# A hybrid decoder step: two small log1p series moved from GpSimd to VectorE, a pair's logarithms issued together, and the planner's lag within an engine set to zero

## The chip, the core and the metric

The kernel runs on one core of a Trainium2 chip. The core has a matrix engine (TensorE; PE in the profile, with its weight loads as PEld), a vector engine (VectorE; DVE), a scalar engine for activation functions (ScalarE; ACT), a general engine (GpSimd; POOL), and a sync engine (SyncE; SP) which here only issues DMAs. Each engine works through its own instructions in program order; they are tied together by semaphores. The metric is the device time of one execution in microseconds (us).

## The reference

One inference step of a two-layer recurrent decoder, for a prompt of 512 tokens and 8 sample tokens, 520 columns in all, width 1024. Layer 0 has two branches, an RG-LRU and a Mamba-2 SSD; layer 1 is an HGRN2. Three places of the reference matter here.

```python
# RG-LRU: constants per channel from a_lam
log_a = -LRU_C * r * jax.nn.softplus(-lam.astype(F32))
a = jnp.exp(log_a)
u = jnp.sqrt(-jnp.expm1(2.0 * log_a)) * (gi * x)
...
# SSD: step sizes per token and head
dt = jax.nn.softplus(b_dt.astype(F32) + b_dt_bias.astype(F32))
acs = jnp.cumsum(dtc * a_neg.reshape(G_B, hg), axis=2)
...
# HGRN2: forget gate and its sums over time
g = jnp.logaddexp(jnp.log(lb), jnp.log1p(-lb) + jax.nn.log_sigmoid(fx))
bcum = jnp.cumsum(gs.reshape(Bsz, H_C, qc, DK_C), axis=2).reshape(Bsz, H_C, ns, ss, DK_C)
```

softplus(x) is max(x, 0) + log1p(exp(-|x|)). The kernel computes the log1p of z = exp(-|x|) by the series 2 (s + s^3/3 + s^5/5 + ... + s^17/17) with s = z / (z + 2).

## The kernel before

All matrix products are made in split single precision: a weight tile and the activations are each cut into a high and a low part (`whi`/`wlo`, `whir`/`wlor`, `xnh`/`xnl`), and three matmuls of 128x128 by 260 columns replace one. A projection tile (128 output rows, 520 columns, 48 matmuls) accumulates in one of two PSUM buffers of the tag `mm`; the next but one tile must wait until an evacuation has emptied it. Everything small goes through four more PSUM banks (`ax`).

Nothing is issued in the order in which it is written. Each call records an operation in a plan (`Plan.record`), with its engine (some copies and scalings may go to ACT or DVE), a cost from a table and a due time: the position of the main matmuls at that place of the program, shifted by `side(...)`. `urgency` pulls the due time of everything that a main matmul depends on to 38.78 us before that matmul. `order` is then a list scheduler: at each step the engine that is free first takes the operation with the earliest due time among those whose predecessors have ended by the cost table. What an operation's end is reckoned to cost its successors is the lag in `release`: `SYNC` (0.12 us) for all but PE to PE, and for PE instructions fed by other engines the spare that `later(...)` sets. `together(...)` puts a gate ahead of a group: no operation of the group is planned before all writes to the named views are done. In hardware the queues run in the planned order, and true dependences wait on semaphores.

The order of the work around the change:

- `norm0` normalizes the input into `xnh`/`xnl`. Behind a gate on the first four tiles of `xnl` come the small tables: `buffers`, `tables` and, later, `dt_tables` and `lower_bounds`.
- `tables` makes the LRU constants. From `a_lam` (8 columns, in `lamt`) ACT takes the absolute value and one exponential at 1/32 of the argument; POOL squares five times (`accurate_exp`), runs the series (`log1p_of`, whose reciprocal alone is on DVE) and makes `c4` and `nc4`.
- The tiles `ax0` to `ax7` are projected. `evac_ax` evacuates each with ACT, convolves it over time on DVE (`conv`), with a POOL and three DVE steps more for the 8 sample columns, and `gates` follows: split `xg`, twelve matmuls `g`, two tanh, then `lt` and `lr`, whose ACT instructions take `nc4` and `c4` as scale and bias. `lru` runs the recurrence on DVE.
- `ssd_start` projects dt (`dt_project`, planned behind `ax7`), takes |dt| and its exponential on ACT, runs the series on 80 columns, and makes `dt` and `dA`. The matmuls `acs` sum `dA` over time. `acsT` goes through DRAM and comes back as `acy`, from which the SSD chunks start. All of `ssd_start` and `lru_out` stands under `later(4.0)`.
- In layer 1 the heads come in eight pairs. For each pair f and v are projected (by a seven-product scheme from the second pair on, tiles `sm` and `sg`), then `decay` for both heads, then q, in the pairs 2, 4 and 6 a chunk of the output projection (`o`), then g. `samples` and `head` of a pair run beside the next pair's projections.
- `decay` takes for each head a logarithm on ACT into `b`, a scan on DVE, eight exponentials on ACT into `qe` and `kd`. Logarithm and exponential lie in different activation tables, so a change between them needs an ACT_TABLE_LOAD. q's evacuation multiplies into `qe` and so waits for the exponentials. `b` of a head lies where the head of the same parity of the previous pair keeps its output `og`; the last readers of that are the cast and the subtraction into `ohl`, at the end of `head`.

In the profile lines, `at__1738` is `at_`, `l1a` is the buffer of `t`, `b`, `kd` and `qe`, and nearly all instructions carry line 520, where the plan issues them, so they are told apart by tile.

Of the kernel before, what the change touches and what calls it, by code (L numbers as in the profile page):

```python
# [29 lines left out]
NH = 16  # L30
# [165 lines left out]
def _meet(a, b):  # L196
    return a[2] < b[3] and b[2] < a[3] and a[0] < b[1] and b[0] < a[1]
# [12 lines left out]
class Plan:  # L210
# [44 lines left out]
        self.spare = keep  # L255

    @contextmanager
    def together(self, *views):

        self.gate = self.barrier([o for v in views for box, o, w in v.buf.acc if w and _meet(box, v.box())])  # L260
        yield
        self.gate = None

# [91 lines left out]
    def order(self):  # L355
# [17 lines left out]
        def release(op, t):  # L373
            todo = [(op, t)]
            while todo:
                p, t_ = todo.pop()
                for s, hard in p.succ:
                    if hard:
                        lag = SYNC if p.forms and not ("pe" in p.forms and "pe" in s.forms) else 0
                        if "pe" in s.forms and p.taken != "pe":  # L380
                            lag += s.spare
                        s.ready = max(s.ready, t_ + lag)
                    s.wait -= 1
                    if not s.wait:
                        offer(s, todo)
# [155 lines left out]
def hybrid_decode_step_kernel(ctx: ExitStack, tc: tile.TileContext, I, O, mode="both"):  # L541
# [44 lines left out]
    def tt(out, a, b, op, eng=dve):  # L586
        eng.tensor_tensor(out=out, in0=a, in1=b, op=op)
# [365 lines left out]
    flag = ctile([1, 1], "flag", I32)  # L953
    fl = ctile([128, 4], "fl")

    def log1p_of(z, n, lo):

        t = htmp[:, lo:lo + 4 * n].rearrange("p (a b) -> p a b", a=4)
        s, s2, q, r = t[:, 0], t[:, 1], t[:, 2], t[:, 3]
        ts(s, z, 2.0, ADD, eng=pool)  # L960
        dve.reciprocal(q, s)
        tt(s, z, q, MUL, pool)
        tt(s2, s, s, MUL, pool)
        ts(q, s2, 1.0 / 17.0, MUL, 1.0 / 15.0, ADD, pool)
        for c in (13, 11, 9, 7, 5, 3, 1):
            tt(q, q, s2, MUL, pool)
            ts(q, q, 1.0 / c, ADD, eng=pool)
        tt(r, q, s, MUL, pool)
        ts(r, r, 2.0, MUL, eng=pool)
        return r  # L970

    def accurate_exp(t, k):

        fn(t, t, AF.Exp, scale=1.0 / (1 << k))
        for _ in range(k):
            tt(t, t, t, MUL, pool)

    def buffers():

# [11 lines left out]
    def tables():  # L991
        pool.memset(triu, 1.0)
        select(triu, [[1, 128]], 0, -1, 0.0)

        act.activation(lamt[:, 0], P1(56, 8), AF.Abs)
        ts(lamt[:, 0], lamt[:, 0], -1.0, MUL, eng=pool)
        accurate_exp(lamt[:, 0], 5)
        l1p_ = log1p_of(lamt[:, 0], 8, 320)
        ts(lamt[:, 1], P1(56, 8), -1.0, MUL, 0.0, MAX, pool)
        tt(lamt[:, 1], lamt[:, 1], l1p_, ADD, pool)  # L1000
        ts(c4, lamt[:, 1], -4.0, MUL, eng=pool)
        ts(nc4, lamt[:, 1], 4.0, MUL, eng=pool)
        ts(hbias, P1(40, 16), 0.5, MUL, eng=pool)
        ts(hcn, P2(64, 16), 0.5, MUL, eng=pool)

        ts(P1(64, 60), P1(64, 60), 0.5, MUL, eng=pool)
# [53 lines left out]
    with plans[-1].together(xnl[:, 3]):  # L1060
        with side(12.0):
            buffers()
            tables()
        with side(25.0):
            dt_tables()
        with side(40.0):
            lower_bounds()
# [157 lines left out]
    def ssd_start():  # L1225
        dt_project()
        act.activation(dt_z, dt_raw, AF.Abs)
        fn(dt_z, dt_z, AF.Exp, scale=-1.0)
        lg_ = log1p_of(dt_z, 80, 0)
        ts(dt, dt_raw, 0.0, MAX, eng=pool)  # L1230
        tt(dt, dt, lg_, ADD, pool)
        tt(dA.rearrange("p (i h) -> p i h", i=5), dt.rearrange("p (i h) -> p i h", i=5),
           bc(aneg.unsqueeze(1), [128, 5, NH]), MUL, pool)
        ps = grab("acs")
        with block():
            pe.matmul(ps[:, 0:64], lhsT=triu, rhs=dA[:, :64], start=True, stop=True)
            pe.matmul(ps[:, 64:128], lhsT=ones, rhs=dA[:, :64], start=True, stop=True)
        copy(at_[:, 0:2, :], ps[:, :128].rearrange("p (a b) -> p a b", a=2))
        ts(nacs[:, :64], acs, -1.0, MUL)
        tt(edt, alast, acs, SUB)  # L1240
        ps = grab("acsT")
        with block():
            pe.transpose(ps[:64, :128], acs, ident)
            pe.transpose(ps[:16, 128:256], dt[:, 64:80], ident)
            pe.transpose(ps[:16, 256:384], dA[:, 64:80], ident)
        copy(acsT, ps[:64, :128])
        copy(sdt[:, 0, :], ps[:16, 248:256])
        fn(sdt[:, 1, :], ps[:16, 376:384], AF.Exp)
        fn(edt, edt, AF.Exp)
        fn(eal, alast, AF.Exp)  # L1250
        sp.dma_start(out=acsT_d, in_=acsT)
        sp.dma_start(out=sdt_d, in_=sdt.rearrange("h a b -> h (a b)"))
        for e in range(2):
            sp.dma_start(out=sfm[e * 64:(e + 1) * 64].rearrange("p j a b -> p j (a b)"),
                         in_=sdt_d.rearrange("(j e) c -> e j c", e=2)[e].partition_broadcast(64))
# [6 lines left out]
                lru(0)  # L1262
    with side(LRU_LATE):
        lru(4)
    with side(DT_LATE), plans[-1].later(4.0):
        ssd_start()
        lru_out()

# [342 lines left out]
    def layer1_fast():  # L1611
# [174 lines left out]

        def decay(hd):

            with plans[-1].together(H[hd]["t"], H[hd + 1]["t"]):
                for e in (hd, hd + 1):  # L1790
                    fn(H[e]["b"][:, :T], H[e]["t"][:, :T], AF.Ln, scale=ch[:, e:e + 1], bias=fb[:, e:e + 1])
            for e in (hd, hd + 1):
                d, p = H[e], e % 2
                b = d["b"][:, :T]
                dve.tensor_tensor_scan(out=b, data0=smask, data1=b, initial=0.0, op0=MUL, op1=ADD)
                b4 = c4v(b)
                last, mid = b4[:, :, CH - 1:CH], b4[:, :, CH // 2 - 1:CH // 2]
                kd, qe = A[:, 2080 + p * T:2080 + (p + 1) * T], A[:, 3104 + p * T:3104 + (p + 1) * T]
                w = small[:, p * 4:p * 4 + 4]
                d.update(kd=kd, qe=qe, w=w)  # L1800
                nm = small[:, 20 + p * 4:24 + p * 4]
                ts(nm.unsqueeze(2), mid, -1.0, MUL)
                for c in range(NCH):
                    cs = slice(c * CH, (c + 1) * CH)
                    fn(qe[:, cs], b[:, cs], AF.Exp, bias=nm[:, c:c + 1])
                    fn(kd[:, cs], b[:, cs], AF.Exp, scale=-1.0, bias=mid[:, c])
                stt(kd, d["t"][:, :T], 1.0, kd, SUB, MUL)
                tt(w.unsqueeze(2), last, mid, SUB)
                tt(w[:, :NCH - 1].unsqueeze(2), w[:, :NCH - 1].unsqueeze(2), mid[:, 1:], ADD)
                fn(w, w, AF.Exp)  # L1810
                ts(w[:, NCH - 1:], w[:, NCH - 1:], cneg[:, e:e + 1], MUL)
# [453 lines left out]
```

## Time and profile before

| | us |
|---|---|
| median of three runs | 1055.54 |
| lowest and highest | 1050.91, 1056.95 |
| profiled execution, device time | 1052.58 |
| its span, first to last instruction | 1050.9 |
| ACT_TABLE_LOAD beside the first, number and each | 36, 1.283 |
| granted TensorE clock, mean over the span | 0.994 |

The profile is of one execution. Timeline rows give start, duration, engine, line, operation, output and inputs with sizes, and in brackets how long the engine stood idle just before and what released it. [...]

### The profile page before, as it was taken

The page shows a single profiled execution, that of the slowest core. Times are in us where ns is not written, and L with a number is a line of the kernel's source. Part 1 is how long each engine was busy: PE and PEld are TensorE (multiplying, and loading weights), DVE is VectorE, ACT ScalarE, POOL GpSimd, SP SyncE. Part 2 cuts the span into 40 slices and gives each one's busy share as a digit, 9 for nine tenths or more (in the row PEclk, how much of TensorE's full clock was granted, in tenths as well). Part 3 has the DMA queues.
Part 4 walks back from the last instruction along what each step waited for, and adds up shares of the span by engine and source line. Part 5 has one row for each costly group of instructions (what it writes and reads, how often), then busy time and mean ns, then how long its engine had stood idle before and what let it go on. Part 6 is the DMA issues. An engine that isn't in the chain of part 4 may idle for free.

```text
span 1050.9 us, 21517 instructions
## 1 busy us (share of the span) xinstructions
PE 1023.1 (97%) x8427; PEld 1000.0 (95%) x8427; DVE 832.6 (79%) x1705; ACT 630.8 (60%) x1482; POOL 139.4 (13%) x241
## 2 busy tenths in 40 slices
PE   9989899999999999999999999999999999999995
PEld 8989899899999999999999999999999999999995
DVE  6789788998996656697989759698598979868853
ACT  6588876654673222365676726678268685764553
POOL 4635854100000000001000000001000000100000
PEclk9999999999999999999999999999999999999998
DMA  9712254336586223553353433433434443553311
GB/s 285 246 30 92 81 166 141 122 110 191 188 257 213 89 98 117 153 203 90 98 149 109 142 91 108 139 100 113 122 90 139 124 116 111 137 180 121 121 41 45
DMA packets 129957, 138.45 MB, mean 132 GB/s; under 512 B 13704, under 2 KB 111128, under 8 KB 129832
## 3 DMA queue, kind: packets, MB, share of 16 engines
q1 hardware_dynamic: 129464, 136.64, 42.6%
q8 instruction: 68, 1.11, 0.4%
q10 hardware_dynamic: 160, 0.30, 0.1%
q14 instruction: 41, 0.34, 0.1%
q0 software_dynamic: 224, 0.06, 0.0%
HBM read 111.71 MB, written 25.44 MB: 131 GB/s over the span
## 4 chain that ended last, share of the span: by engine, by line
PE 73%; DVE 10%; DMA 6%; ACT 4%; POOL 3%; issue 2%; SPq 0%; POOLq 0%; ACTq 0%; DVEq 0%
PE o L520 10%; PE sm L520 9%; PE q L520 9%; PE pg L520 9%; PE g L520 8%; PE ob L520 4%; PE sg L520 4%; PE xbc L520 2%; PE ax L520 2%; DVE wlo L520 2%; PE oa L520 2%; PE pl L520 2%; PE z L520 1%; DMA smp<-in_state_b_ssm_dram 1%; POOL csm L520 1%
## 5 line engine op out<-in xcount | busy, mean ns | idle before, releaser
L520 ACT CAST whir<-wraw 128x512 fp32r<-128x512 f32 (+1 forms) x121 | 96.3, 798 | 83.9 <-PE o L520 40.6
L520 DVE TENSOR_TENSOR wlor<-wraw,whir 128x512 fp32r<-128x512 f32 (+1 forms) x121 | 109.6, 910 | 12.5 <-ACT whir L520 12.1
L520 ACT CAST whi<-wraw 128x1024 fp32r<-128x1024 f32 (+1 forms) x56 | 57.8, 1032 | 48.6 <-PE ob L520 34.5
L520 POOL TENSOR_TENSOR at__1738<-at__1738,nhalf 128x4 f32<-128x4 f32 (+1 forms) x24 | 22.6, 942 | 461.5 <-DVE at__1738 L520 455.5
L520 DVE TENSOR_TENSOR wlo<-wraw,whi 128x1024 fp32r<-128x1024 f32 (+1 forms) x64 | 77.3, 1208 | 8.0 <-ACT whi L520 7.4
L520 PE MATMUL o<-ohl,whir 128*128 128x260 f32 x512 | 83.0, 284 | 0.0
L520 PEld LDWEIGHTS o<-ohl,whir 128*128 128x128 f32 x512 | 70.0, 188 | 0.9 <-issue 0.6
L520 PE MATMUL g<-xh,whir 128*128 128x260 f32 x256 | 54.6, 294 | 1.1 <-DVE l1a L520 1.1
L520 PE MATMUL q<-xh,whir 128*128 128x260 f32 x256 | 53.2, 289 | 0.0
L520 PE MATMUL q<-xh,wlor 128*128 128x260 f32 x256 | 51.5, 283 | 0.0
L520 PE MATMUL q<-xl,whir 128*128 128x260 f32 x256 | 51.4, 282 | 0.0
L520 PE MATMUL g<-xl,whir 128*128 128x260 f32 x256 | 51.4, 282 | 0.0
L520 PE MATMUL g<-xh,wlor 128*128 128x260 f32 x256 | 51.4, 282 | 0.0
L520 PE MATMUL o<-ohl,wlor 128*128 128x260 f32 x256 | 51.4, 282 | 0.0
L520 DVE TENSOR_TENSOR h<-h,o 128x520 f32<-128x520 f32 x40 | 27.8, 694 | 26.2 <-PE o L520 25.9
L515 ACT ACT_TABLE_LOAD x36 | 46.2, 1283 | 0.6
L520 PE MATMUL sm<-uh,whir 128*128 128x260 f32 x140 | 40.4, 289 | 1.8 <-DVE l1a L520 1.6
L520 PE MATMUL sm<-xh,whir 128*128 128x260 f32 x140 | 41.4, 296 | 0.0
L520 PEld LDWEIGHTS g<-xh,whir 128*128 128x128 f32 x256 | 39.2, 189 | 2.2 <-DVE l1a L520 1.3
L520 PE MATMUL sm<-xh,wlor 128*128 128x260 f32 x140 | 39.6, 283 | 0.3 <-DVE wlor L520 0.3
L520 PE MATMUL xbc<-xnh,whi 128*128 128x260 f32 x192 | 39.7, 289 | 0.0
L520 PE MATMUL sm<-xl,whir 128*128 128x260 f32 x140 | 39.6, 283 | 0.0
(609 smaller groups left out, 3594.2 us busy)
## 6 DMA issues: line engine op xcount, KB each, us to landing
wraw<-in_c_w_in_dram SPq DMA_DIRECT2D x32, 1024.0 KB
wraw<-in_ab_w_in_dram SPq DMA_DIRECT2D x15, 1024.0 KB
wraw<-in_ab_w_out_dram SPq DMA_DIRECT2D x8, 1024.0 KB
wraw<-in_ple_gate_dram SPq DMA_DIRECT2D x8, 1024.0 KB
wraw<-in_c_w_out_dram SPq DMA_DIRECT2D x8, 1024.0 KB
pl<-pl_d SPq DMA_DIRECT2D x2, 2080.0 KB
smp<-in_state_b_ssm_dram SPq DMA_DIRECT2D x8, 512.0 KB
acy<-acsT_d SPq DMA_DIRECT2D x8, 512.0 KB
```

The lines of the kernel that those rows point to most:

```text
L515: self.engines["act"].preload_act_table_set(SETS[table])
L520: getattr(f, name)(*a, **k)
```

## The change

Three edits, the first with two settings beside it. First, the two series go to DVE and get a shorter form, in which one `scalar_tensor_tensor` makes a step of the polynomial; the maximum, the sum with the series, `c4` and `nc4`, the five squarings of the LRU constants and the product `dA` go to DVE as well. `tables` gets an earlier due time (4.0 for 12.0), and `ssd_start` with `lru_out` a smaller spare (2.0 for 4.0). Second, `decay`'s gate takes in the readers of the two buffers `b`, so both logarithms of a pair wait for the same point. Third, the lag in `release` is zero where an operation and its successor have the same engine and the successor has no other. The squarings of the other two `accurate_exp` calls stay on POOL.

```diff
-    def together(self, *views):
+    def together(self, *views, over=()):
 
-        self.gate = self.barrier([o for v in views for box, o, w in v.buf.acc if w and _meet(box, v.box())])
+        self.gate = self.barrier([o for v in views for box, o, w in v.buf.acc if w and _meet(box, v.box())]
+                                 + [o for v in over for box, o, w in v.buf.acc if _meet(box, v.box())])
...
-                        lag = SYNC if p.forms and not ("pe" in p.forms and "pe" in s.forms) else 0
+                        lag = SYNC if p.forms and (p.taken not in s.forms or len(s.forms) > 1) else 0
...
-    def log1p_of(z, n, lo):
-        t = htmp[:, lo:lo + 4 * n].rearrange("p (a b) -> p a b", a=4)
-        s, s2, q, r = t[:, 0], t[:, 1], t[:, 2], t[:, 3]
-        ts(s, z, 2.0, ADD, eng=pool)
-        dve.reciprocal(q, s)
-        tt(s, z, q, MUL, pool)
-        tt(s2, s, s, MUL, pool)
-        ts(q, s2, 1.0 / 17.0, MUL, 1.0 / 15.0, ADD, pool)
-        for c in (13, 11, 9, 7, 5, 3, 1):
-            tt(q, q, s2, MUL, pool)
-            ts(q, q, 1.0 / c, ADD, eng=pool)
-        tt(r, q, s, MUL, pool)
-        ts(r, r, 2.0, MUL, eng=pool)
-        return r
+    def softplus_tail(dst, z, n, lo):
+        t = htmp[:, lo:lo + 3 * n].rearrange("p (a b) -> p a b", a=3)
+        s, s2, r = t[:, 0], t[:, 1], t[:, 2]
+        ts(s2, z, 2.0, ADD)
+        dve.reciprocal(r, s2)
+        tt(s, z, r, MUL)
+        tt(s2, s, s, MUL)
+        ts(r, s2, 1.0 / 17.0, MUL)
+        for c in (15, 13, 11, 9, 7, 5, 3):
+            stt(r, r, 1.0 / c, s2, ADD, MUL)
+        stt(r, r, 1.0, s, ADD, MUL)
+        stt(dst, r, 2.0, dst, MUL, ADD)
...
-    def accurate_exp(t, k):
+    def accurate_exp(t, k, eng=pool):
...
-            tt(t, t, t, MUL, pool)
+            tt(t, t, t, MUL, eng)
...
-        ts(lamt[:, 0], lamt[:, 0], -1.0, MUL, eng=pool)
-        accurate_exp(lamt[:, 0], 5)
-        l1p_ = log1p_of(lamt[:, 0], 8, 320)
-        ts(lamt[:, 1], P1(56, 8), -1.0, MUL, 0.0, MAX, pool)
-        tt(lamt[:, 1], lamt[:, 1], l1p_, ADD, pool)
-        ts(c4, lamt[:, 1], -4.0, MUL, eng=pool)
-        ts(nc4, lamt[:, 1], 4.0, MUL, eng=pool)
+        ts(lamt[:, 0], lamt[:, 0], -1.0, MUL)
+        accurate_exp(lamt[:, 0], 5, dve)
+        ts(lamt[:, 1], P1(56, 8), -1.0, MUL, 0.0, MAX)
+        softplus_tail(lamt[:, 1], lamt[:, 0], 8, 320)
+        ts(c4, lamt[:, 1], -4.0, MUL)
+        ts(nc4, lamt[:, 1], 4.0, MUL)
...
             buffers()
+        with side(4.0):
             tables()
...
-        lg_ = log1p_of(dt_z, 80, 0)
-        ts(dt, dt_raw, 0.0, MAX, eng=pool)
-        tt(dt, dt, lg_, ADD, pool)
+        ts(dt, dt_raw, 0.0, MAX)
+        softplus_tail(dt, dt_z, 80, 0)
         tt(dA.rearrange("p (i h) -> p i h", i=5), dt.rearrange("p (i h) -> p i h", i=5),
-           bc(aneg.unsqueeze(1), [128, 5, NH]), MUL, pool)
+           bc(aneg.unsqueeze(1), [128, 5, NH]), MUL)
...
-    with side(DT_LATE), plans[-1].later(4.0):
+    with side(DT_LATE), plans[-1].later(2.0):
...
-            with plans[-1].together(H[hd]["t"], H[hd + 1]["t"]):
+            with plans[-1].together(H[hd]["t"], H[hd + 1]["t"], over=(H[hd]["b"], H[hd + 1]["b"])):
```

## The prediction

> **What bounds the kernel now.** I read the page first (busy shares), then a table by stretches, then the waits and the timelines of the places where TensorE stands still.
>
> ```profile
> PE 1023.1 (97%) x8427; PEld 1000.0 (95%) x8427; DVE 832.6 (79%) x1705; ACT 630.8 (60%) x1482; POOL 139.4 (13%) x241
> ...
> 26.00:45.00 19.00, 18.39 (x149) 17.61 (x148) 15.00 (x25) 10.69 (x21) 10.78 (x26) 1.00 0.65 223
> 45.00:62.00 17.00, 13.93 (x108) 12.94 (x107) 12.15 (x34) 10.74 (x21) 11.83 (x30) 1.00 0.40 136
> 62.00:88.00 26.00, 26.00 (x217) 25.81 (x216) 25.17 (x52) 25.03 (x41) 9.27 (x15) 1.00 0.22 61
> 105.00:128.00 23.00, 19.73 (x165) 19.53 (x164) 15.79 (x20) 20.25 (x28) 21.18 (x45) 1.00 0.29 93
> 450.00:985.00 535.00, 531.42 (x4407) 522.00 (x4406) 439.29 (x996) 349.18 (x855) 27.67 (x33) 1.00 0.41 122
> ```
>
> The columns of the table are stretch, length, then busy time (and count) of PE, PEld, DVE, ACT, POOL, then clock, DMA share, GB/s. TensorE is busy for 97% of the span, so an edit on another engine is worth only what TensorE stands still for it. The stretches that the change touches hold three such places: 17.00 - 13.93 = 3.07 us in 45 to 62, 23.00 - 19.73 = 3.27 us in 105 to 128, and 3.58 us in the whole of layer 1 (450 to 985). In the first two POOL is busy for 11.83 and 21.18 us, far above its 13% share of the span.
>
> **The LRU constants (3.0 us).** The timelines of POOL, ACT, DVE and PE, in that order:
>
> ```profile
> 54.75 1.22 POOL L520 TENSOR_SCALAR lamt<-lamt 128x8 f32<-128x8 f32 x2
> ...
> 56.00 0.82 ACT L520 ACTIVATE lt<-lr,lamt 128x520 f32<-128x520 f32 x1 [4.33 <-POOL lamt L520]
> ...
> 51.75 0.25 DVE L520 SCALAR_TENSOR_TENSOR xa<-htmp,pt,xa 128x8 f32<-128x8 f32 x1 [2.90 <-POOL xa L520]
> 58.39 0.75 DVE L520 SCALAR_TENSOR_TENSOR lt<-vtmp,lt 128x520 f32<-128x520 f32 x1 [1.75 <-ACT vtmp L520]
> ...
> 48.33 1.58 PE L520 MATMUL g<-xg,gw 128*128 128x260 f32 x11 [0.37 <-DVE xg L520]
> 55.27 1.59 PE L520 MATMUL g<-xg,gw 128*128 128x260 f32 x11 [1.63 <-DVE xg L520]
> 59.71 0.36 PE L520 MATMUL g<-xg,gw 128*128 128x260 f32 x1 [0.71 <-DVE xg L520]
> 60.35 1.59 PE L520 MATMUL g<-xg,gw 128*128 128x260 f32 x11 [0.29 <-DVE xg L520]
> ```
>
> c4 and nc4 (in `lamt`) come out of a POOL chain of 30 small steps that ends at 54.75 + 1.22 = 55.97. ACT's first gate stands 4.33 us for it. POOL's small conv steps for the sample rows queue in the same engine, and DVE stands 2.90 us for one of them; 1.75 us more are handed on from ACT. The gate matmuls `g` then wait for the split `xg` that DVE makes late: 0.37 + 1.63 + 0.71 + 0.29 = 3.00 us, which is the 3.07 of the table. With the chain gone from POOL and finished early, both causes go. What is late next is DVE's own conv work, back to back; I take the whole 3.0, with 1.9 (only the waits at 55 and the small ones after it, 0.7 left standing) to 4.0 (also DVE's idle time before 45) as bounds.
>
> **The dt chain (4.8 us).** POOL, then PE, then one row of the table by stretches:
>
> ```profile
> 104.08 2.00 POOL L520 TENSOR_SCALAR dtt<-dtt 128x80 f32<-128x80 f32 x1 [5.09 <-DVE dtt L520]
> ...
> 127.46 0.36 POOL L520 TENSOR_TENSOR dtt<-dtt,hb 128x80 f32<-128x80 f32 x1
> ...
> 123.97 0.40 PE L520 MATMUL xbc<-xnl,whi 128*128 128x260 f32 x2
> 124.21 0.40 PE L520 MATMUL xbc<-xnh,wlo 128*128 128x260 f32 x2
> 127.88 0.43 PE L520 MATMUL acs<-dtt,triu 128*128 128x64 f32 x2 [3.27 <-POOL dtt L520]
> ...
> 130.05 0.64 PE L520 MATMUL xbc<-xnh,whi 128*128 128x260 f32 x2
> 130.48 0.64 PE L520 MATMUL xbc<-xnl,whi 128*128 128x260 f32 x2
> ...
> 128.00:150.00 22.00, 22.00 (x172) 21.96 (x173) 19.98 (x32) 12.58 (x32) 14.66 (x19) 0.92 0.42 129
> ```
>
> 23 POOL steps run from 104.08 to 127.82, interleaved with other small POOL work, and the matmul `acs` stands in TensorE's queue for the last of them: 3.27 us. Behind the stall the clock falls: 0.92 over 22 us is 22 x 0.08 / 0.5 = 3.5 us at half rate, and a pair of matmuls takes 130.48 - 130.05 = 0.43 us there against 124.21 - 123.97 = 0.24 us before. That loses 3.5 x (1 - 0.24/0.43) = 1.55 us. Stall and clock together are 4.8 us. [...]
>
> **What DVE gets instead.** Prices from the DVE and ACT timelines:
>
> ```profile
> 44.00 2.73 DVE L520 SCALAR_TENSOR_TENSOR xa<-bcs,pt,xa 128x512 f32<-128x512 f32 x4
> 46.65 0.22 DVE L520 SCALAR_TENSOR_TENSOR xa<-htmp,pt,xa 128x8 f32<-128x8 f32 x1
> 46.78 0.74 DVE L520 SCALAR_TENSOR_TENSOR xa<-bcs,pt,xa 128x512 f32<-128x512 f32 x1
> ...
> 102.94 0.23 DVE L520 TENSOR_TENSOR dtt<-dtT,hb 128x80 f32<-128x80 f32 x1
> 103.09 0.74 DVE L520 SCALAR_TENSOR_TENSOR bcs<-bcs,pt 128x512 f32<-128x512 f32 x1
> ...
> 106.68 0.65 DVE L520 RECIPROCAL htmp<-htmp 128x80 f32<-128x80 f32 x1 [0.88 <-POOL htmp L520]
> ...
> 34.90 0.21 ACT L520 ACTIVATE lamt<-lamt 128x8 f32<-128x8 f32 x1
> ...
> 105.04 0.26 ACT L520 ACTIVATE dtt<-dtt 128x80 f32<-128x80 f32 x1
> ```
>
> From start to start a step of 8 columns takes 0.13 us (46.65 to 46.78), one of 80 columns 0.15 us (102.94 to 103.09). A step may follow the one it needs at no extra price: the four conv steps from 44.00, among them such as build on the one before, take (46.65 - 44.00)/4 = 0.66 us each. LRU: 1 + 5 squarings + 1 + 14 of the series + 2 = 23 steps, one of them (the reciprocal) on DVE already: 22 x 0.13 = 2.9 us. dt: 1 + 14 + 1 = 16, again 15 of them new: 15 x 0.15 = 2.3 us. DVE has 4.0 and 4.85 us idle in 26 to 45 and 45 to 62, and 7.2 in 105 to 128, so I cost both at nothing; with that cover gone they cost up to 5.2 us. They come in time: the LRU series starts at the latest behind the exponential at 34.90 + 0.21 and needs about 3.2 us, so it ends near 38.4, 13 us before ACT asks (56.00 - 4.33 = 51.7). dt starts behind 105.30; 0.65 + 2.3 us make it 108.2, or 118 if a conv step of 0.66 us slips in between each two, both well before 127.9. The cut of the planned spare from 4.0 to 2.0 us can put a PE instruction up to 2.0 us too early at the few hand-overs of this part (nothing to 2.0; I take nothing, since DVE's short steps are steadier than the POOL ones, of which one took 2.00 us). [...]
>
> **The decay's logarithms.** A group row of ACT, DVE and ACT rows of pair 1 in order of time, PE's g, and two ACT rows of pair 3:
>
> ```profile
> L515 ACT ACT_TABLE_LOAD x36 | 46.2, 1283 | 0.6
> ...
> 529.57 0.69 DVE L520 TENSOR_TENSOR ohl<-l1a,ohl 128x520 fp32r<-128x520 f32 x1
> 531.75 0.81 ACT L520 ACTIVATE l1a<-l1a,lbt 128x512 f32<-128x512 f32 x1
> 537.31 0.88 DVE L520 SCALAR_TENSOR_TENSOR l1a<-q,lbt,l1a 128x260 f32<-128x260 f32 x2
> 539.65 0.69 DVE L520 TENSOR_TENSOR ohl<-l1a,ohl 128x520 fp32r<-128x520 f32 x1
> 540.66 0.82 ACT L520 ACTIVATE l1a<-l1a,lbt 128x512 f32<-128x512 f32 x1
> 546.17 0.88 DVE L520 SCALAR_TENSOR_TENSOR l1a<-q,lbt,l1a 128x260 f32<-128x260 f32 x2
> ...
> 542.77 0.40 PE L520 MATMUL g<-xh,whir 128*128 128x260 f32 x2
> ...
> 663.76 0.81 ACT L520 ACTIVATE l1a<-l1a,lbt 128x512 f32<-128x512 f32 x1
> ...
> 680.29 0.81 ACT L520 ACTIVATE l1a<-l1a,lbt 128x512 f32<-128x512 f32 x1
> ```
>
> Each logarithm follows the last read (`ohl`) of the buffer that the previous pair's head of the same parity leaves it: 531.75 behind 529.57, 540.66 behind 539.65. The gate makes both wait for the later one. It saves two table loads in each of seven pairs, 14 x 1.283 = 18 us of ACT; ACT is busy 349 of 535 us there, so this is off the path. What it can cost: behind the first logarithm stand its scan, eight exponentials and the evacuation of q's PSUM, and that buffer is taken by `g` at 542.77. If the previous head's tail stays at 539.65, that evacuation moves from 537.31 to about 546.2 and `g` waits 3.4 us. But the planner ranks each step by the matmul that hangs on it, and that tail now hangs on a matmul one tile of q (some 6 us) earlier, so it should come forward by about as much, to near 534; then q is out before 541. Pair 3, with 16.5 us between its logarithms, has least room. I take 1.0 us slower for this part, between 3.6 faster (all idle time of layer 1) and the rival below.
>
> **No semaphore time within an engine** changes the planned order of every part by 0.12 us steps. DVE's rows bear the new figure out. I take nothing, within 2 us either way.
>
> **Sum.** -3.0 - 4.8 + 1.0 = -6.8 us. The profiled execution took 1052.58 us (span 1050.9), the three runs 1050.91 to 1056.95; I set the sum against the median: 1055.5 - 6.8 = 1048.7 us (1045.8 against the profiled one).
>
> **Rivals.** (1) *The gate turns into a wait of TensorE.* The price is the 3.4 us of pair 1 in seven pairs, 24 us, and 35 if each stall also drags the half clock behind it as the one at 124 did (7 x 1.55 more). Less the 7.8 gained this gives 1072 to 1083; if the tails come only halfway forward, about 1060. It decides from the point at which the tail gains less than about 3.4 us of the 6. For it: 16.5 us between the logarithms of pair 3; against: ACT is relieved of 18 us just there. (2) *DVE takes the place of POOL.* From 62 to 88 DVE is busy 25.17 and ACT 25.03 of 26 us, so a TensorE that arrives 3 us sooner may find its work not ready, and the 5.2 us of new DVE work show: 1055.5 - 7.8 + 5.2 = 1052.9. (3) *More is gained:* the ACT time freed takes copies off DVE and the 3.6 us idle in layer 1 go too: 1055.5 - 7.8 - 3.6 = 1044.1. That the edits do not act at all is hardly possible, since both waits name POOL's own tiles.
>
> **How the numbers follow.** Forecast 0.50 (four fifths of it over the bound), (3) 0.15, (2) 0.17, (1) 0.18, most of it halfway. About 0.5% (5.3 us, so 1050.3) is what can be told from no change. Faster 0.40 + 0.15 = 0.55; same 0.10 + 0.17 + 0.02 = 0.29; slower 0.16. The range runs from below (3), 1042, past (2) to the halfway case of (1), 1062, and leaves out the full (1) and a little below.
>
> **What would show it.** Right: ACT's wait for `lamt` and the `g` waits at 45 to 62 gone, no PE wait for `dtt` and a clock of 1.00 from 128 to 150, 22 or 23 table loads, the two logarithms of a pair next to each other. Wrong: `g` or `o` matmuls waiting for DVE `l1a` behind q, or `g` waits for `xg` between 62 and 105.

## The result and the profile after

The changed kernel takes 1068.65 us in the median (1067.16 to 1069.83, 4 runs), the kernel before beside it 1055.01 (1050.91 to 1056.95, 4 runs). The ratio is 1.0134, with a 95% interval of 1.0100 to 1.0167: about 13.6 us slower, where 6.8 us faster was forecast, and outside the range of 1042 to 1062.

First the busy line of the page after, then rows of its table by stretches (stretch, length, busy time and count of PE, PEld, DVE, ACT, POOL, clock, DMA share, GB/s):

```profile
PE 1027.6 (96%) x8427; PEld 1002.2 (94%) x8427; DVE 852.5 (80%) x1740; ACT 619.2 (58%) x1468; POOL 108.4 (10%) x188
```

```profile
45.00:62.00 17.00, 16.23 (x136) 16.02 (x135) 16.44 (x37) 8.83 (x15) 3.69 (x4) 1.00 0.61 209
...
105.00:128.00 23.00, 22.95 (x193) 22.71 (x192) 20.06 (x40) 16.92 (x33) 8.21 (x20) 1.00 0.17 49
128.00:150.00 22.00, 17.91 (x136) 17.50 (x135) 19.00 (x29) 12.43 (x22) 11.81 (x19) 0.92 0.54 171
```

Where the forecast saw idle time go, it went. In 45 to 62 TensorE stands still for 0.77 us (3.07 before) and in 105 to 128 for 0.05 (3.27 before), and POOL falls from 11.83 and 21.18 us busy to 3.69 and 8.21. (The stretches are the same times, not quite the same work: the first `ax` matmul starts at 30.18 us, at 26.85 before.) But 128 to 150 now lacks 22.00 - 17.91 = 4.09 us and has a mean clock of 0.92 again: behind the wait of 2.41 us at 142.69 below, the stretch 143 to 145 has 0.50. The head of the view of TensorE's waits (who waits for what, microseconds in total, times, longest), the three waits of its timeline from 99 to 180 us, and the group of the table loads on ACT:

```profile
PE sm L521 <- DVE l1b L521: 5.5, 7, 1.1
PE os L521 <- DVE l1d L521: 3.9, 8, 0.7
```

```profile
102.88 0.60 PE L521 MATMUL g<-xg,gw 128*128 128x260 f32 x3 [2.21 <-DVE dtt L521]
131.12 0.51 PE L521 MATMUL xbc<-xnh,wlo 128*128 128x260 f32 x2 [1.67 <-DVE wlo L521]
142.69 0.30 PE L521 MATMUL ah<-ident,ahs 128*72 128x128 f32 x1 [2.41 <-POOL ahs L521]
```

```profile
L516 ACT ACT_TABLE_LOAD x20 | 25.7, 1283 | 0.3
```

None of these waits stood in the prediction. Two kinds are to be told apart: small ones that come back with nearly every pair of layer 1 (`sm` behind `l1b` seven times, `os` behind `l1d` eight times), and large single ones in layer 0. The decay part did what it was to do: 20 table loads for 36 (22 in gate_only and no_lag, which keep the old lag). The two logarithms of a pair now follow each other directly, as one row of ACT's timeline (pair 1):

```profile
542.82 1.52 ACT L521 ACTIVATE l1a<-l1a,lbt 128x512 f32<-128x512 f32 x2
```

### The profile page after: what moved, and what is told of

Same layout as the page of the kernel before. It is cut to its first block, busy times and chain, and to the rows that moved or that the text cites. A ratio compares the mean times of both kernels' runs of the same rounds, so it can differ in the third digit from the quotient of the medians.

```text
span 1067.7 us, 21470 instructions
## 1 busy us (share of the span) xinstructions
PE 1027.6 (96%) x8427; PEld 1002.2 (94%) x8427; DVE 852.5 (80%) x1740; ACT 619.2 (58%) x1468; POOL 108.4 (10%) x188
## 4 chain that ended last, share of the span: by engine, by line
PE 64%; DVE 23%; ACT 3%; issue 3%; DMA 3%; POOL 3%; SPq 0%; DVEq 0%; ACTq 0%; POOLq 0%
PE o L521 9%; PE q L521 9%; PE pg L521 8%; PE sm L521 7%; PE ag L521 4%; PE ob L521 4%; PE z L521 4%; PE sg L521 4%; DVE l1d L521 3%; DVE xa L521 2%; DVE wlo L521 2%; PE g L521 2%; DVE wlor L521 2%; DVE sqt L521 2%; PE pl L521 2%
## 5 line engine op out<-in xcount | busy, mean ns | idle before, releaser
L521 POOL TENSOR_TENSOR at__1559<-at__1559,nhalf 128x4 f32<-128x4 f32 (+1 forms) x24 | 20.4, 861 | 465.6 <-DVE at__1559 L521 465.6
L521 PE MATMUL xbc<-xnh,wlo 128*128 128x260 f32 x192 | 39.5, 288 | 1.7 <-DVE wlo L521 1.7
L521 PE MATMUL sm<-ul,whir 128*128 128x260 f32 x140 | 39.7, 283 | 0.0
## 6 DMA issues: line engine op xcount, KB each, us to landing
smp<-in_state_b_ssm_dram SPq DMA_DIRECT2D x8, 512.0 KB
acy<-acsT_d SPq DMA_DIRECT2D x8, 512.0 KB
```

The costliest lines, as they stand in the source:

```text
L521: getattr(f, name)(*a, **k)
```

## The experiments

**Which part costs.** Each part of the change was put alone into the kernel before, and the lag was undone in the changed kernel (`no_lag`: series and gate with the old lag of 0.12 us, in spite of its name).

```diff
 # lag_only: the kernel before with this line alone; no_lag: the changed kernel without it
-                        lag = SYNC if p.forms and not ("pe" in p.forms and "pe" in s.forms) else 0
+                        lag = SYNC if p.forms and (p.taken not in s.forms or len(s.forms) > 1) else 0
 # gate_only: the kernel before with this edit alone
-            with plans[-1].together(H[hd]["t"], H[hd + 1]["t"]):
+            with plans[-1].together(H[hd]["t"], H[hd + 1]["t"], over=(H[hd]["b"], H[hd + 1]["b"])):
 # series_only: both series on DVE, side(4.0) and later(2.0), with the old gate and the old lag
```

Expected:

> The kernel before with nothing but the new lag rule. If the rule is the cause (a re-ordered plan loses in the start-up and in layer 1), 8 to 14 us slower than before, with the first ax matmul some 3 us late and sm matmuls of layer 1 waiting for DVE. If the gate is the cause, within 3 us of before. If the series on DVE is the cause, within 3 us of before.

> The kernel before with both series on DVE, the earlier due time of the tables and the spare of 2.0; old lag, old gate. By the prediction's sum 7.8 us faster than before. If the series is the cause of the loss, 3 to 8 us slower, with gate matmuls g waiting for xg between 62 and 105. If the lag or the gate is the cause, 3 to 8 us faster.

> The kernel before with nothing but the wider gate of the decay. If the gate is the cause, 6 to 24 us slower, all of it in layer 1, with g or sm matmuls waiting for DVE l1a. By the prediction 1 us slower. If the lag is the cause, within 3 us of before, with 22 or so table loads.

> The changed kernel with the old lag rule: series and gate together. If the lag is the cause, 3 to 7 us faster than before. If the gate is, as slow as the changed kernel or nearly (6 us or more slower than before). If the three parts simply add up, its difference from before is that of series_only plus that of gate_only, within 2 us.

Measured, with the kernel before at 1057.44 us in the same comparison (21 runs):

| kernel | median us | ratio to before (95%) |
|---|---|---|
| lag_only | 1070.00 | 1.0117 (1.0074 to 1.0159) |
| series_only | 1051.15 | 0.9940 (0.9919 to 0.9960) |
| gate_only | 1059.22 | 1.0006 (0.9986 to 1.0026) |
| no_lag | 1049.98 | 0.9918 (0.9891 to 0.9946) |

The lag is the whole loss. Without it the change is faster than the kernel before, as forecast; alone it costs 12.6 us (1070.00 - 1057.44), and on top of the rest 1068.65 - 1049.98 = 18.7 us. These two medians come from different comparisons; each set against the kernel before beside it, the difference is 13.64 + 7.46 = 21.1 us, so differences between comparisons are good to some 3 us. Two expectations failed in part. The parts don't simply add up: series_only and gate_only together gain 6.3 - 1.8 = 4.5 us, no_lag gains 7.5, 3 us apart instead of within 2. And the first `ax` matmul of lag_only starts at 27.60 us, 0.75 late and not 3; no_lag has it at 29.59, so the late start isn't the lag's.

**What a dependent step costs.** The rows that tell this are in the traces of these kernels. DVE's timeline of the changed kernel, three conv steps of one chain taken singly with the step behind them, and seven steps of the dt series:

```profile
98.08 0.76 DVE L521 SCALAR_TENSOR_TENSOR xa<-bcs,pt,xa 128x512 f32<-128x512 f32 x1
98.88 0.75 DVE L521 SCALAR_TENSOR_TENSOR xa<-bcs,pt,xa 128x512 f32<-128x512 f32 x1
99.67 0.75 DVE L521 SCALAR_TENSOR_TENSOR xa<-bcs,pt,xa 128x512 f32<-128x512 f32 x1
100.34 0.69 DVE L521 SCALAR_TENSOR_TENSOR lt<-vtmp,lt 128x520 f32<-128x520 f32 x1
...
110.44 1.97 DVE L521 SCALAR_TENSOR_TENSOR htmp<-htmp 128x80 f32<-128x80 f32 x7
112.45 0.24 DVE L521 SCALAR_TENSOR_TENSOR dtt<-htmp,dtt 128x80 f32<-128x80 f32 x1
```

A conv step that needs the one before starts 0.80 and 0.79 us after it (98.08 to 98.88 to 99.67); `lt`, which doesn't, 0.67 us after. The steps of 80 columns stand (112.45 - 110.44)/7 = 0.29 us apart. The prediction priced the two at 0.66 and 0.15. (Some expectations below say 0.09 us for the long step: that was the mean over the three rows, the last of which is followed by an independent step. Singly it is 0.13.) A conv chain and the dt series in no_lag:

```profile
103.96 0.74 DVE L521 SCALAR_TENSOR_TENSOR bcs<-bcs,pt 128x512 f32<-128x512 f32 x1
104.62 0.23 DVE L521 SCALAR_TENSOR_TENSOR htmp<-htmp 128x80 f32<-128x80 f32 x1
104.77 0.74 DVE L521 SCALAR_TENSOR_TENSOR bcs<-bcs,pt 128x512 f32<-128x512 f32 x1
105.44 0.23 DVE L521 SCALAR_TENSOR_TENSOR htmp<-htmp 128x80 f32<-128x80 f32 x1
```

With 0.12 us of lag the planner finds the next step of a chain not ready and slips a step of the other chain in between: 0.66 us behind the long step, 0.15 behind the short one, and the price is gone. With the lag at zero it runs each chain straight through and pays between every two steps. The same in layer 1, in the chains of the sample rows (`samples`: a state column in `sqt`, then a sum in `l1d` that needs it), where the changed kernel comes first and no_lag second:

```profile
563.53 0.35 DVE L521 SCALAR_TENSOR_TENSOR sqt<-l1d,sqt 128x128 f32<-128x128 f32 x1
563.91 0.35 DVE L521 SCALAR_TENSOR_TENSOR l1d<-sqt,l1d 128x128 f32<-128x128 f32 x1
564.18 0.34 DVE L521 SCALAR_TENSOR_TENSOR sqt<-l1d,sqt 128x128 f32<-128x128 f32 x1
```

```profile
553.91 0.35 DVE L521 SCALAR_TENSOR_TENSOR l1d<-sqt,l1d 128x128 f32<-128x128 f32 x1
554.17 0.35 DVE L521 SCALAR_TENSOR_TENSOR sqt<-l1d,sqt 128x128 f32<-128x128 f32 x1
554.43 0.35 DVE L521 SCALAR_TENSOR_TENSOR l1d<-sqt,l1d 128x128 f32<-128x128 f32 x1
554.70 0.35 DVE L521 SCALAR_TENSOR_TENSOR sqt<-l1d,sqt 128x128 f32<-128x128 f32 x1
```

After the change a sum follows its own column 0.38 us from start to start (563.53 to 563.91) and the next column 0.27 later: 0.65 us for the two. In no_lag a sum and a column that don't need each other alternate, every step is 0.26 or 0.27 us behind the one before, and the two take 0.53. All durations are the same 0.35 us; only the distance of the starts tells. So the kernel before had it nearly right for DVE: a step right behind the one it needs costs 0.13 us more at 128x512, 0.12 at 128x128 and 0.14 at 128x80. Where one independent step stands in between, as in no_lag's rows from 103.96, nothing of it is left.

**Which engine, and which value.** All on the base of no_lag; only the lag between a step and a successor that has the same engine alone is changed.

```diff
 # dve_zero: 0 from DVE to DVE; act_zero: 0 from ACT to ACT; dve_act_zero: both
+                        lag = ... and not (p.taken == "dve" and list(s.forms) == ["dve"]) else 0
 # lag_half: 0.06, lag_double: 0.24; lag_10 and lag_13: 0.10 and 0.13, on DVE and ACT only
+                        lag = (0.5 * SYNC if p.taken in s.forms and len(s.forms) == 1 else SYNC) if ... else 0
 # fitted: by the rows as they were read then
+                        if p.taken == "dve" and list(s.forms) == ["dve"]:
+                            lag = 0.09 if p.forms["dve"][1] > 0.4 else 0.14
+                        elif p.taken == "act" and list(s.forms) == ["act"]:
+                            lag = 0.13
 # charged: 0 from DVE to DVE as in dve_zero, but the price is added to the step
+                if e == "dve":
+                    if behind in op.preds:
+                        c += SYNC
+                    behind = op
```

Expected:

> The changed kernel with the old lag, except that a step of DVE which can only run on DVE is reckoned ready at once when the step before it ran on DVE too (ACT, POOL and the queues keep 0.12 us). Theory A (a step that follows the one it needs costs DVE 0.09 to 0.14 us more than the plan now reckons, so chains stand back to back and everything behind them comes late): most of the 18 us between no_lag and the changed kernel is DVE's, 1060 to 1068 us. Theory B (any change of the lag reshuffles the order by chance): anywhere from 1045 to 1070. Theory C (it is ACT's chains): 1050 to 1054.

> The same with ACT in place of DVE: only a step of ACT behind a step of ACT is reckoned without the 0.12 us. Theory A: ACT is busy 619 of 1068 us and its dependent steps cost 0.13 us more (0.85 against 0.72), but few of them stand in chains: 1050 to 1057 us. Theory B: anywhere from 1045 to 1070. Theory C: 1060 to 1068.

> The changed kernel with the lag between steps of one engine doubled to 0.24 us, and 0.12 us between engines. Theory A: the plan then reckons more than the 0.09 to 0.14 us that the rows show; it puts another step in between where one is ready, which costs nothing: 1046 to 1055 us, as no_lag within 5 us. Theory B: a reshuffle like that of the zero lag, 1055 to 1070 as likely as not.

> The changed kernel with 0.06 us between steps of one engine. Theory A: half of the price is missing, so some of the 18 us is lost, 1052 to 1062 us. A variant of A, in which only the order of two ready steps counts and not the sum: 0.06 us is enough to let the independent step go first, 1048 to 1053. Theory B: anywhere from 1045 to 1070.

> The changed kernel with the lag within an engine set to what the rows show: on DVE 0.09 us behind a step reckoned at over 0.4 us and 0.14 us behind a shorter one, on ACT 0.13 us; 0.12 us everywhere else. Theory A (a plan that reckons the dependent step as the chip runs it loses nothing): 1045 to 1053 us, no_lag or a little better. Theory B (any change of the lag reshuffles the order by chance, and 0.12 us was only the value that the other constants were set for): 1052 to 1065 as likely as not.

> The changed kernel with the old lag, but on DVE the 0.12 us are no longer time in which a dependent step isn't ready: it is ready at once, and where it does follow the step it needs the plan adds 0.12 us to its length. So the plan knows the price, and no longer puts an independent step in between for it. Theory A1 (the loss is that the plan reckons DVE too early, and TensorE's order is set too early with it): the price is known again, 1048 to 1055 us. Theory A2 (the loss is DVE's own time, since back-to-back steps leave the price unfilled): DVE busy stays near 855 us, against 836 of no_lag, and the time is 1057 to 1066.

> The changed kernel with 0.12 us left only on POOL and the queues. If POOL's dependent steps carry the rest of the loss: as dve_zero, 1060 to 1064. If DVE's and ACT's zero lag together do: as the changed kernel, 1066 to 1070.

> no_lag with 0.13 us between two steps of DVE and between two steps of ACT, the price that single rows show, in place of 0.12. If a plan with the true price loses nothing: 1047 to 1053 us, layer 1 as long as in no_lag (512.0 us). If layer 0 is open to any small change of the lag: layer 1 still at 512 to 513 us, but the end of layer 0 anywhere from 433 to 441 us and the time from 1048 to 1058.

> no_lag with 0.10 us there, a little under the price. If a small error of the lag costs in proportion (0.06 us cost 6 us): 1051 to 1053 us. If layer 1 holds as long as the plan still puts other steps in between, and layer 0 is open to any small change: layer 1 at 512 to 513 us, the end of layer 0 from 433 to 441, the time from 1048 to 1058.

Measured; DVE busy is from each page, the length of layer 1 from the last `pg` to the last `g` matmul of each trace (no_lag: 435.90 to 947.91, changed kernel: 446.68 to 964.67):

| kernel | median us | before beside it | ratio (95%) | DVE busy | end of `pg` | layer 1 |
|---|---|---|---|---|---|---|
| no_lag | 1049.98 | 1057.44 | 0.9918 (0.9891 to 0.9946) | 836.4 | 435.9 | 512.0 |
| lag_10 | 1048.81 | 1055.95 | 0.9937 (0.9915 to 0.9960) | 837.6 | 434.7 | 509.5 |
| act_zero | 1049.29 | 1057.88 | 0.9929 (0.9902 to 0.9957) | 835.5 | 433.8 | 512.5 |
| fitted | 1057.27 | 1054.83 | 1.0025 (1.0003 to 1.0047) | 835.1 | 440.4 | 512.0 |
| lag_13 | 1058.68 | 1055.95 | 1.0024 (1.0008 to 1.0040) | 835.5 | 443.9 | 511.7 |
| lag_half | 1055.89 | 1057.88 | 0.9995 (0.9979 to 1.0011) | 838.1 | 436.8 | 517.1 |
| dve_zero | 1062.43 | 1057.88 | 1.0046 (1.0027 to 1.0065) | 855.6 | 439.4 | 518.3 |
| dve_act_zero | 1062.85 | 1055.75 | 1.0071 (1.0045 to 1.0096) | 852.5 | 439.7 | 517.6 |
| changed kernel | 1068.65 | 1055.01 | 1.0134 (1.0100 to 1.0167) | 852.5 | 446.7 | 518.0 |
| lag_double | 1063.86 | 1057.88 | 1.0075 (1.0048 to 1.0103) | 837.1 | 436.0 | 523.1 |
| charged | 1069.63 | 1054.83 | 1.0167 (1.0127 to 1.0206) | 851.0 | 433.1 | 530.9 |

Two busy lines show what the fifth column means; the page of no_lag, then that of dve_zero:

```profile
PE 1023.5 (97%) x8427; PEld 998.9 (95%) x8427; DVE 836.4 (80%) x1756; ACT 611.6 (58%) x1454; POOL 122.8 (12%) x188
```

```profile
PE 1026.1 (97%) x8427; PEld 1000.9 (94%) x8427; DVE 855.6 (81%) x1753; ACT 612.9 (58%) x1455; POOL 108.9 (10%) x188
```

The same work keeps DVE busy 19 us longer once its own lag is zero. All kernels with zero lag on DVE lie at 851 to 856, all the others of this table at 835 to 838. The starts in layer 1 say why: of the `scalar_tensor_tensor` steps of 128x128, 16 of 272 in no_lag have the next DVE step 0.36 to 0.40 us behind them, the distance of a dependent step, but 95 of 268 in dve_zero and 92 of 280 in the changed kernel. ACT's lag alone costs nothing (act_zero, 1049.29 us for no_lag's 1049.98). The rest, 5.8 us from dve_act_zero to the changed kernel, came with the lag of POOL and the queues; it lies in layer 0 (layer 1 takes 517.6 and 518.0 us), and no single wait was isolated for it.

act_zero came out 0.7 us under its 1050; dve_zero came out where theory A had it, and dve_act_zero like dve_zero, as expected if POOL and the queues carry the rest. **lag_half** has a time inside theory A's range, but not for theory A's reason, so the hit is luck. Its gaps are filled (DVE busy 838.1, and only 20 of 273 steps in layer 1 with the long distance), and yet its layer 1 is 517.1 us long, almost as long as with zero lag. Its largest wait there, behind a step of ACT, comes six times for no_lag's three:

```profile
PE sg L521 <- ACT whir L521: 3.7, 6, 0.6
```

So unfilled distances aren't the only way in which a wrong lag loses; the order can go wrong without them. lag_double, fitted and lag_13 missed theory A's ranges, and lie in those of theory B, a reshuffle, or just above (lag_13). **lag_double** was to lose nothing and lost 14 us. Its largest wait in layer 1 (450 to 1000 us), then the two largest of no_lag and of dve_zero:

```profile
PE sg L521 <- DVE l1a L521: 8.2, 6, 1.6
```

```profile
PE sg L521 <- ACT whir L521: 1.8, 3, 0.6
PE sg L521 <- DVE l1a L521: 0.5, 3, 0.2
```

```profile
PE os L521 <- DVE l1d L521: 3.8, 5, 1.0
PE sm L521 <- DVE l1b L521: 3.8, 5, 0.9
```

Zero lag makes the sample chains and the step behind them late (`l1d`, `l1b`). Doubled lag makes another step late. DVE and PE of lag_double at the first such wait, then DVE of no_lag at the same place:

```profile
517.77 0.68 DVE L521 TENSOR_TENSOR wraw<-wraw,v1s 128x512 f32<-128x512 f32 x1
518.38 0.61 DVE L521 SCALAR_TENSOR_TENSOR l1c<-l1d,l1c 128x128 f32<-128x128 f32 x2
518.90 0.34 DVE L521 SCALAR_TENSOR_TENSOR l1d<-l1c,l1d 128x128 f32<-128x128 f32 x1
519.17 0.68 DVE L521 TENSOR_TENSOR wlor<-wraw,whir 128x512 fp32r<-128x512 f32 x1
519.77 0.34 DVE L521 SCALAR_TENSOR_TENSOR l1d<-l1c,l1d 128x128 f32<-128x128 f32 x1
...
520.17 0.41 DVE L521 TENSOR_TENSOR l1a<-l1a,sg 128x260 f32<-128x260 f32 x1
```

```profile
520.64 0.39 PE L521 MATMUL sg<-uh,whir 128*128 128x260 f32 x1 [1.56 <-DVE l1a L521]
```

```profile
518.03 0.68 DVE L521 TENSOR_TENSOR wraw<-wraw,v1s 128x512 f32<-128x512 f32 x1
518.63 0.34 DVE L521 SCALAR_TENSOR_TENSOR l1d<-l1c,l1d 128x128 f32<-128x128 f32 x1
...
519.04 0.42 DVE L521 TENSOR_TENSOR l1a<-l1a,sg 128x260 f32<-128x260 f32 x1
```

In no_lag `l1a` starts 1.01 us after `wraw` (518.03 to 519.04). In lag_double three more steps of the sample chains and a weight split stand in front of it, and it is 2.40 us (517.77 to 520.17). Too much lag is an error of the plan as well; it makes another step late. **charged** loses in the same place, the `sg` matmuls behind `l1a`:

```profile
PE sg L525 <- DVE l1a L525: 13.3, 6, 2.6
```

So knowing the price isn't enough; the planner also has to put something else into the gap. Charged, with the price in the sum but nothing put in between for it, has DVE at 851.0 and the longest layer 1 of all. That is what theory A2 asked for, though with a larger loss than it gave (1069.6, over its 1066); why `sg` waits longer there than in any other kernel was not followed further.

**fitted** was to show that the price as read then loses nothing, and missed by 4 us; **lag_13**, with the price of the single rows, misses its 1047 to 1053 by 6. In layer 1 both do what the theory asks: they are as long as no_lag there to 0.3 us. They lose in layer 0, where their timelines of TensorE have the same two large waits, fitted first:

```profile
33.79 0.80 PE L525 MATMUL ax<-xnh,wax 128*128 128x260 f32 x2 [5.18 <-ACT htmp L525]
143.88 0.43 PE L525 MATMUL ah<-ident,ahs 128*72 128x128 f32 x1 [4.52 <-POOL ahs L525]
```

```profile
33.78 0.80 PE L523 MATMUL ax<-xnh,wax 128*128 128x260 f32 x2 [5.34 <-ACT htmp L523]
143.86 0.43 PE L523 MATMUL ah<-ident,ahs 128*72 128x128 f32 x1 [3.10 <-POOL ahs L523]
```

lag_double has the first too, with 3.76 us at 34.85. These three have more than 0.12 us between steps of ACT; in the kernels with 0.12 or less no `ax` wait there is longer than 2.3 us. But lag_double doesn't have the second, and its layer 0 ends at 436.0 us, as early as that of no_lag. So the first wait alone doesn't make layer 0 late; the second, which no_lag hasn't either, goes with it in both late kernels. The order of layer 0 turns at such places on a hundredth of a microsecond, while layer 1 doesn't: lag_10, lag_13, fitted and no_lag lie between 509.5 and 512.0 us there. lag_13 is also 0.7 us over the 1058 of its second theory, and its layer 0 ends at 443.9 instead of at most 441. lag_10 came out 2 us below what its first theory gave; time and end of layer 0 are inside the second, and its layer 1 is 2.5 us shorter than the 512 that this had. From 0.10 to 0.13 us layer 0 ends anywhere from 434 to 444 us, so one such run says nothing of the price; the length of layer 1, where eight like pairs repeat, does.

**The two layers apart.** Zero lag was put in one layer only (by the number of operations recorded before layer 1 starts):

```diff
+    plans[-1].cut = len(plans[-1].ops)
     layer1_fast()
 # layer1_zero; layer0_zero has s.i < self.cut
+                        if s.i >= self.cut and p.taken in s.forms and len(s.forms) == 1:
+                            lag = 0
```

> The changed kernel with the old lag in layer 0 and the new one in layer 1. If the loss of layer 1 follows the lag (the dependent steps of the samples' chains, 0.38 us from start to start against 0.26): 5 to 7 us over no_lag, 1055 to 1057, with TensorE waiting for l1b and l1d in layer 1 as in the changed kernel. If the loss is all of layer 0: 1049 to 1051.

> The changed kernel with the new lag in layer 0 and the old one in layer 1. If the 10.8 us by which the profiled changed kernel stands behind no_lag at the end of layer 0 belong to its order: 1058 to 1063. If they were a mishap of that one profiled execution: 1050 to 1055.

Measured 1058.22 us (1.0027, 1.0011 to 1.0043) for layer1_zero and 1060.40 (1.0037, 1.0020 to 1.0054) for layer0_zero, with before at 1055.75. Over no_lag these are 8.2 and 10.4 us, together 18.6, against the 18.7 of the changed kernel (each set against the kernel before beside it: 9.9 and 12.1, together 22.0, against 21.1). The first lies a little over its 5 to 7 us. DVE busy is 844.3 and 843.8, half of the rise each. Layer 1 is 518.4 us long in layer1_zero and 512.0 in layer0_zero. The waits of layer1_zero in layer 1, then TensorE's timeline of layer0_zero:

```profile
PE sm L524 <- DVE l1b L524: 5.5, 7, 1.1
PE os L524 <- DVE l1d L524: 4.3, 8, 1.1
```

```profile
100.75 0.60 PE L524 MATMUL g<-xg,gw 128*128 128x260 f32 x3 [2.22 <-DVE dtt L524]
...
129.13 0.51 PE L524 MATMUL xbc<-xnh,wlo 128*128 128x260 f32 x2 [1.66 <-DVE wlo L524]
140.70 0.43 PE L524 MATMUL ah<-ident,ahs 128*72 128x128 f32 x1 [2.42 <-POOL ahs L524]
```

Each half brings back its own waits of the changed kernel to some hundredths of a microsecond (2.22, 1.66 and 2.42 for 2.21, 1.67 and 2.41). These are properties of the order, not mishaps of one execution.

**Is DVE's new work really hidden?** Both series were run twice in no_lag, first into a scratch tile that the second has to wait for, so the kernel does part of its work twice:

```diff
+        ts(htmp[:, 240:320], dt_raw, 0.0, MAX)
+        softplus_tail(htmp[:, 240:320], dt_z, 80, 0)
         softplus_tail(dt, dt_z, 80, 0)
```

and the same for the LRU constants, with 8 columns.

> no_lag with both series run twice in a row, the first time into a scratch tile, so that the second waits for it: 15 steps of 80 columns and 15 of 8 more on DVE (the reciprocals and one step for each scratch sum among them), some 5 to 7 us of DVE busy time in 26 to 62 and 105 to 128 us. If DVE's new work lies in its idle time, as the forecast has it: within 2 us of no_lag, 1048 to 1052. If it is on the path: all of it shows, 1055 to 1058.

Measured 1050.80 us (1049.01 to 1053.23; 0.9954, 0.9935 to 0.9974, before at 1054.83). That is 0.8 us from no_lag by the medians; set against the kernel before beside each it is 3.4 us (7.46 - 4.03), but the two intervals overlap. DVE's busy time didn't rise by the 5 to 7 us that were expected: it is 836.2, with 22 instructions more on DVE and 6 more on ACT, to which the planner can give some copies. The `ah` matmul waits 3.71 us behind POOL at 150.41, which it doesn't in no_lag, but all idle time of TensorE from 20 us to the end of `pg` is 6.8 us there (417.28 - 410.50) and 7.1 in no_lag (415.90 - 408.79). So the work is hidden, up to the 3 us by which two comparisons can differ.

The best kernels are no_lag, act_zero and lag_10, which the intervals don't tell apart: 1048.8 to 1050.0 us, 0.6 to 0.8% faster than the kernel before and some 19 us faster than the changed one. The simplest of them is no_lag, the change without its third edit.

## Why the prediction was wrong

- **The LRU constants and the dt chain** (-7.8 us): right in size, and half right in the path. Alone they bring 6.3 us (1057.44 - 1051.15), with the 7.8 inside the interval (0.0040 to 0.0081 of 1057.44, 4.2 to 8.6 us). TensorE's waits that were named went, and in series_only the clock of 128 to 150 is 1.00, as the sum had it. (The prediction took the half clock from one case, the wait of 3.27 us before 127.88. The length of the one wait doesn't tell: in the changed kernel 2.41 us before 142.69 was followed by 0.50 from 143 to 145, but 2.21 us before 102.88 by 1.00 from 103 to 105. In series_only, behind 2.23 us before 28.77, the pairs of matmuls stand 0.43 us apart (30.67 to 31.10) and the mean clock from 26 to 45 is 0.91; lag_half has 0.91 there too, behind only 1.90 us before 34.68.)

```profile
45.00:62.00 17.00, 17.00 (x144) 17.00 (x143) 16.19 (x50) 10.38 (x19) 3.45 (x5) 1.00 0.62 213
...
105.00:128.00 23.00, 23.00 (x195) 22.96 (x194) 22.96 (x40) 18.82 (x33) 17.97 (x27) 1.00 0.26 74
128.00:150.00 22.00, 20.90 (x173) 20.61 (x172) 15.93 (x26) 17.90 (x42) 9.39 (x13) 1.00 0.58 194
```

The dt chain went as forecast: `acs` starts at 114.75 us in series_only and waits for nothing. The LRU constants didn't. The forecast had them near 38.4 us, 13 us before ACT asks. With the old lag their last step, here DVE's row in series_only, comes later than POOL's before (54.75 + 1.22 = 55.97), as longer work goes between the short steps:

```profile
56.65 0.24 DVE L521 TENSOR_SCALAR lamt<-lamt 128x8 f32<-128x8 f32 x2
```

ACT takes them at 59.68 us without a wait, where it took them at 56.00 before. (In the changed kernel they do end early, at 45.36.) So early constants aren't what freed TensorE from 45 to 62 in series_only, and that this part of the forecast came out is partly luck. What did get shorter in these 17 us is DVE's waiting: for POOL's `xa` 0.56 us instead of 2.90 and 0.20, behind ACT's `vtmp` nothing instead of 1.75.

- **What DVE gets instead** (nothing): right in the sum as far as series_twice can tell, wrong in the price of a step. In the changed kernel seven steps of the dt series take 0.29 us each, not 0.15.
- **The decay's logarithms** (+1.0 us): not to be told from it. gate_only is 0.06% slower, with an interval of 0.14% faster to 0.26% slower; on top of the series it is 1.2 us faster. Rival 1 did not come: no wait of the changed kernel over 0.5 us is a `g` of layer 1 or behind q. Of table loads 20 stayed, not the 22 or 23 named; with the old lag 22 did.
- **No semaphore time within an engine** ("I take nothing, within 2 us either way. DVE's rows bear the new figure out"): this is the step that failed, and with it the sign. It costs 12.6 us alone and 18.7 here. It rests on one reading: "A step may follow the one it needs at no extra price: the four conv steps from 44.00". Those four were taken for one chain. The row groups them and leaves out the tiles: they are steps of two tiles in turn, each needs the one before last, and 0.66 us is the price of a step that waits for nothing; the conv steps of one tile stand 0.79 and 0.80 us apart in the changed kernel. The steps of 80 columns show the same: in the dt series of the changed kernel the dependent ones stand 0.29 us apart, recorded as 0.24 us long, and in no_lag, recorded as 0.23 us long, one is followed by an independent step after 0.15 us.
- **The rivals** looked at the gate, at DVE's load and at more gain; none was the plan itself. Of the sign of rival 2, `g` behind DVE between 62 and 105, the changed kernel has 0.55 us at 78.66 and 2.21 at 102.88, no_lag 0.79 at 93.97; its 5.2 us for DVE's new work don't show in series_twice. What came instead: a lag that the cost table needs is taken out, chains close up, DVE pays the unfilled distance and what stands behind them comes late. The bound of 2 us was too small by far: DVE's busy time alone is 16.1 us over no_lag's (852.5 - 836.4).

What stays open: the 10.8 us of layer 0 (446.7 - 435.9) are not divided between closed-up chains and single hand-overs that turned out badly, as the two of fitted did; what the lag of POOL and the queues does there was not tried alone. In layer 1 the closed-up chains and the late `l1b` and `l1d` are shown together, but how much of the 6.0 us (518.0 - 512.0) the distances cost by themselves isn't: lag_half fills them and loses 5.1 us there all the same.

## What to carry to other kernels

A lag in a list scheduler (a planner that always takes the most urgent ready step) does two things: it says when a result is there, and it decides whether an independent step is put in between; taking it out as mere semaphore time, as the prediction did, lost both here (18.7 us over no_lag). Before pricing a step as free behind the one it needs, find in the trace two steps that certainly depend on each other (same tile in and out, one column count) and compare the distance of their starts with that of two that don't. And an edit that reorders the whole program gets a range of its own, from the spread of such orders, not the 2 us of a local edit: here kernels with the same work lay between 1049 and 1070 us.

## What the runs showed of the hardware

- A DVE step (`scalar_tensor_tensor`) that needs the one directly before it started 0.79 us after it at 128x512, 0.38 at 128x128 and 0.29 at 128x80 (changed kernel, from 98.88, 563.53 and 110.44); one that doesn't, 0.66, 0.26 and 0.15 us after it (no_lag, from 103.96, 553.91 and 104.62). That is 0.12 to 0.14 us at these three widths. The recorded durations hardly show it: 0.75 and 0.74 us, 0.35 and 0.35, 0.24 and 0.23. With one independent step in between, all of it was hidden: no_lag's two chains from 103.96 alternate at 0.66 and 0.15 us.
- The busy time of an engine wasn't given by its instructions alone: nearly the same DVE work (1756 and 1753 instructions) reads 836.4 us in no_lag and 855.6 us in dve_zero, in another order.
- The half clock of TensorE didn't follow the length of the one wait before it: 0.50 came behind 2.41 us (changed kernel, 143 to 145) and 1.00 behind 2.21 us (changed kernel, 103 to 105), but a mean clock of 0.91 from 26 to 45, with no wait there over 1.90 us, in lag_half.
